# A routing table built with four short VectorE operations per step instead of ScalarE work, and one expert choice that is advanced later

## The chip, the cores and the metric

The kernel runs on one core of a Trainium2 chip. What is measured is device time in microseconds (us), from one launch, on that core; the number compared is the median of three runs. A core has TensorE (PE in the rows below, with PEld for its weight loads), VectorE (DVE), ScalarE (ACT), GpSimd (POOL) and SyncE (SP); each works through its own queue of instructions in order, and they meet at semaphores. SP and POOL issue the DMAs here. Weights and inputs lie in HBM (DRAM), tiles in SBUF, matmul results in PSUM.

## The reference

One decoder layer over 1024 tokens of width 1024. A mixer (gated short convolution, and dilated window attention with 24 heads) is followed by a mixture of 16,384 small experts; the change lies in the second part:

```
def peer_ffn(u, w_query, sub_keys, expert_down, expert_up):
    q = (xf @ w_query).reshape(T, PEER_HEADS, 2, PEER_D_HALF)
    s = jnp.einsum('thcd,hckd->thck', q, sub_keys)
    top_s, top_i = lax.top_k(s, PEER_TOPK)
    cand_s = top_s[:, :, 0, :, None] + top_s[:, :, 1, None, :]
    cand_i = top_i[:, :, 0, :, None] * PEER_N_KEYS + top_i[:, :, 1, None, :]
    best_s, pos = lax.top_k(cand_s, PEER_TOPK)
    idx = jnp.take_along_axis(cand_i, pos, axis=-1)
    gates = jax.nn.softmax(best_s, axis=-1)
    # for each chunk of tokens:
    a = jax.nn.gelu(jnp.einsum('cd,ced->ce', xc, expert_down[ic]), approximate=False)
    return jnp.einsum('ce,ced->cd', gc * a, expert_up[ic])
```

For each token, 8 heads each pick 16 of 16,384 experts. An expert is a row of expert_down (a dot product with the token) and a row of expert_up (added with weight gate times gelu). All of it is float32.

## The kernel before, in words

The 1024 tokens are two halves of 512, and eight tiles of 128. A projection in float32 is three matmuls: each operand is split into a high part (`hi`, rounded by ACT at L165 or L181) and a rest (`lo`, a subtraction on DVE at L167 or L182), and `mm3` (L176 to L178) multiplies hi*hi, hi*lo and lo*hi. So each 512 KB of weights costs one ACT operation and one DVE operation ahead of 24 matmuls of 512 columns.

**The two halves treat the experts differently.** The first half (tiles 0 to 3) gathers rows: `experts()` goes through `STEPS`, (tile, 0) for the down rows and (tile, 1) for the up rows, in the order (0,0), (1,0), (2,0), (0,1), (1,1), (2,1), (3,0), (3,1). A step takes 128 gathers by POOL (L885 or L908), each of one 512 KB block (for 128 tokens, one expert row each) into one of four buffers, and for each gather one DVE operation (L887: dot product; L908's is L910: multiply and add into `acc`). Step (0,1) is different (`summed`): its rows are summed by TensorE (`upacc`, L944) and need no DVE operation per row. In this text this chain is the side chain, and one gather with its DVE operation is a row. The second half (tiles 4 to 7) does not gather: it multiplies by all experts (`dense`). For this it needs a table `g_d` in DRAM that holds, for each token, the gate at each expert that it chose, and zero elsewhere.

**The stages.** Half 0's mixer; half 1's mixer (`mixer(1)`: attention with its projections, the joining of its three groups at L551 to L559, the gates' projections at L611, the merge with `w_attn_out`, `w_conv_out`, `w_out`, then `tail` with the queries); then `dense`: first ten blocks of `hidden` (projection by expert_down and gelu) beside the building of the table; then the main loop of 32 blocks `q`: `weigh(q)` reads the table back as `gg` and multiplies (L1056), and the result is multiplied by the rows of expert_up into PSUM (`held`, `psu`). The last block normalises and writes the output (L1150, L1154, L855). The side chain runs beside all this from half 1's mixer on.

**The choice.** `choose` finds, for one tile of 128 tokens, the experts and gates: 16 columns of scores with MAX, MAX_INDEX and MATCH_REPLACE (L762 to L766), then candidates, ranks and names (L776 to L828), some 174 DVE operations. It is run for eight tiles. `later[1]` to `later[3]` are those of tiles 1 to 3, which the side chain needs before step (t,0). `CHOOSE` = (0, 1, 2, 3) says which of them is advanced where in half 1's mixer: after each head pair of attention group 1 that of tile 1, in group 2 that of tile 2, and in the merge that of tile 3. The columns of a stored tile are read by DMAs that stand in POOL's queue (L839).

**The table.** `build` makes it for one of half 1's tiles, 4 tokens per step, 32 steps per tile, 128 in all. In a step, `oa` (DVE, L1025) marks for 4 tokens which of 128 first keys each choice has; `ob` marks the second key, times the gate; `psg` (TensorE, 4 products) is the table's part for the 4 tokens; ACT copies it into `stg` (L1040, four copies of 128x128), and after 8 steps SP writes 2 MB to `g_d` (four DMAs, L1044). `ob` is made in one of two ways in turn: in even steps ACT takes Abs per token (L1029, four), Relu over all (L1030) and DVE multiplies by the gate (L1031); in odd steps DVE compares (L1033) and ACT multiplies by the gate per token (L1036, four).

**What sets the order.** The program is recorded from generators: the stage's main generator yields amounts of work, and the side chain and the builder are advanced by them (`PACE_B`, `PACE_C`, `PACE_D`, `RATE_G`). A scheduler then orders each engine's instructions from its own estimates, so that the written order is only a tendency. The order that it gives is fixed in the program.

Of the kernel before, what the change touches and what calls it, by code (L numbers as in the profile page):

```python
# [8 lines left out]
F32 = mybir.dt.float32  # L9
# [4 lines left out]
ALU = mybir.AluOpType  # L14
# [28 lines left out]
OBUF = 4  # L43
# [3 lines left out]
CHOOSE = (0, 1, 2, 3)  # L47
# [9 lines left out]
STG = 5  # L57
# [8 lines left out]
def hybrid_layer(ctx, tc, x, xT, pos, rotc, norm_mix, w_proj, w_v, conv_w, w_conv_out, w_attn_out,  # L66
# [805 lines left out]
    def experts():  # L872
        values, turned = {}, {}
        for tt, side_up in STEPS:
# [28 lines left out]
            else:  # L903
                acc = ex.tile([P, D], F32, tag="acc", name="acc")
                SIDE.dma_start(acc, h1_d[r])
                for e in range(P):
                    row = new_row("rowu")
                    G.indirect_dma_start(out=row, out_offset=None, in_=up,  # L908
                                         in_offset=bass.IndirectOffsetOnAxis(ap=idx[:, e:e + 1], axis=0))
                    V.scalar_tensor_tensor(acc, row, a[:, e:e + 1], acc, op0=ALU.mult, op1=ALU.add)  # L910
                    yield 1.0
# [59 lines left out]
    def dense():  # L971
# [28 lines left out]
        def chosen(tt):  # L1000
            if tt == 0:
                yield from later[ORDER[3]]
# [8 lines left out]
        def build(srcs, c0):  # L1011
# [5 lines left out]
                for c in range(c0, c0 + P // TC):  # L1017
                    stg = [den.tile([P, 32, TC], F32, tag="stg", bufs=STG, name="stg") for _ in range(4)]
                    for t4 in range(TC // 4):
# [7 lines left out]
                        if t4 % 2 == 0:  # L1027
                            for t in range(4):
                                S.activation(ob[:, t], iota, AF.Abs, bias=i2[:, t:t + 1], scale=-1.0)  # L1029
                            S.activation(ob, ob, AF.Relu, bias=ones[:, 0:1], scale=-1.0)  # L1030
                            V.tensor_tensor(ob, ob, gv[:, :, None].to_broadcast([P, 4, P]), op=ALU.mult)  # L1031
                        else:
                            V.tensor_tensor(ob, iota[:, None, :].to_broadcast([P, 4, P]),  # L1033
                                            i2[:, :, None].to_broadcast([P, 4, P]), op=ALU.is_equal)
                            for t in range(4):
                                S.mul(ob[:, t], ob[:, t], gv[:, t:t + 1])  # L1036
                        for t in range(4):
                            PE.matmul(ps[:, t], ob[:, t], oa[:, t], start=True, stop=True)  # L1038
                        for w in range(4):
                            S.copy(stg[w][:, :, t4 * 4:t4 * 4 + 4],  # L1040
                                   ps[:, :, 32 * w:32 * w + 32].rearrange("p t i -> p i t"))
                        yield 1.1
                    for w in range(4):
                        nc.sync.dma_start(g_d[c, :, 32 * w:32 * w + 32], stg[w])  # L1044
# [30 lines left out]
        for _ in builder:  # L1075
            yield 0.0
        while "done" not in place:
            next(side)
# [155 lines left out]
```

## Time and profile before

| | |
|---|---|
| median of three runs | 3437.81 us (3435.53 to 3441.62) |
| the profiled execution | 3448.45 us, of which 3446.7 us lie between its first and last instruction |
| PE busy | 3165.5 us (92%) |
| DVE busy | 2669.4 us (77%) |
| ACT busy | 1398.0 us (41%) |
| POOL busy | 1422.7 us (41%) |
| HBM read and written | 885.61 MB and 70.32 MB, 277 GB/s over the span |

Busy shares are means over stages with different limits, so they are read stage by stage: the view of busy time by stretch shows which engine leaves no gap, the view of waits shows who waited for whom there, and the rows of groups give what one instruction of a kind takes. [...]

### The profile page before, as it was taken

Reading aid. Unit: us, or ns where it says so; the run is one execution under the profiler, and the core shown is the slowest. Engines: PE = TensorE matmul, PEld = TensorE weight load, DVE = VectorE, ACT = ScalarE, POOL = GpSimd, SP = SyncE. Lnnn points to the kernel's source line nnn. Section 1 sums busy time; section 2 is a strip of 40 time slices with the busy share of each in tenths; the row PEclk is TensorE's granted clock in tenths of the full one; section 3 lists DMA queues with packets and bytes.
Section 4 is the critical chain, followed back from the end, with each engine's and each line's share of the span. In section 5 each row is a group of like instructions: output and inputs, shape, how many; then the busy total and the mean of one; then the engine's idle time right before and its main releaser. Section 6 shows DMA issues by size and latency. Waiting matters only on the chain.

```text
span 3446.7 us, 45451 instructions
## 1 busy us (share of the span) xinstructions
PE 3165.5 (92%) x15410; PEld 2559.9 (74%) x15410; DVE 2669.4 (77%) x5357; ACT 1398.0 (41%) x2898; POOL 1422.7 (41%) x1101
## 2 busy tenths in 40 slices
PE   7999999999899997979779985699999999999996
PEld 6788788887677875768556764588887878778775
DVE  5333455799999989888987748888887878778887
ACT  3544444543344362333465678332322232222222
POOL 0000000024555455555555334455555656555555
PEclk9999999999999997989889997799999999999998
DMA  4233345778888888999888887999999999999997
GB/s 131 77 118 115 95 136 201 237 251 308 295 297 306 306 304 276 344 321 338 307 295 328 322 316 280 335 341 329 324 347 327 333 330 329 327 322 336 322 318 276
DMA packets 349225, 965.26 MB, mean 280 GB/s; under 512 B 35264, under 2 KB 118720, under 8 KB 346432
## 3 DMA queue, kind: packets, MB, share of 16 engines
q0 software_dynamic: 152064, 551.62, 44.6%
q1 hardware_dynamic: 196928, 410.74, 35.0%
q8 instruction: 121, 1.98, 0.2%
q14 instruction: 112, 0.92, 0.1%
HBM read 885.61 MB, written 70.32 MB: 277 GB/s over the span
## 4 chain that ended last, share of the span: by engine, by line
PE 29%; DMA 16%; issue 14%; DVE 12%; POOL 9%; ACT 2%; SPq 1%; POOLq 0%; DVEq 0%; ACTq 0%
DMA rowu<-in_up,idx 7%; POOL row L885 6%; PE ps L178 5%; PE ps L176 5%; PE ps L177 5%; DMA row<-in_down,idx 4%; DVE row L887 4%; POOL rowu L908 3%; PE held L176 2%; PE held L177 2%; PE held L178 2%; PE psg L1038 2%; DVE lo L167 1%; PE upacc L944 1%; DVE acc L910 1%
## 5 line engine op out<-in xcount | busy, mean ns | idle before, releaser
L885 POOL DMA_INDIRECT row<-in_down,idx x512 | 668.9, 1306 | 670.9 <-DVE a L887 331.2
L908 POOL DMA_INDIRECT rowu<-in_up,idx x384 | 559.1, 1456 | 456.9 <-DVE acc L910 392.8
L165 ACT CAST hi<-raw 128x1024 fp32r<-128x1024 f32 x368 | 387.0, 1052 | 788.3 <-PE ps L177 491.7
L887 DVE CUSTOM_DVE_ANT_0 row<-row,ut 128x1024 f32<-128x1024 f32 x512 | 618.1, 1216 | 94.9 <-DMA row<-in_down,idx 89.3
L167 DVE TENSOR_TENSOR lo<-raw,hi 128x1024 fp32r<-128x1024 f32 x368 | 449.0, 1220 | 259.7 <-ACT hi L165 246.8
L910 DVE SCALAR_TENSOR_TENSOR acc<-rowu,a,acc 128x1024 f32<-128x1024 f32 x384 | 492.4, 1282 | 141.6 <-DMA rowu<-in_up,idx 132.1
L178 PE MATMUL ps<-vhi,lo 128*128 128x512 f32 (+1 forms) x1408 | 531.4, 377 | 29.1 <-DVE lo L167 27.4
L176 PE MATMUL ps<-vhi,hi 128*128 128x512 f32 (+1 forms) x1408 | 527.3, 375 | 5.8 <-ACT ga L989 3.6
L177 PE MATMUL ps<-vlo,hi 128*128 128x512 f32 (+1 forms) x1408 | 526.7, 374 | 0.1
L176 PE MATMUL ps<-uhi,hi 128*128 128x512 f32 x1024 | 407.0, 399 | 7.8 <-ACT hi L165 5.3
L178 PE MATMUL ps<-uhi,lo 128*128 128x512 f32 x1024 | 407.7, 399 | 2.0 <-DVE lo L167 1.9
L177 PE MATMUL ps<-ulo,hi 128*128 128x512 f32 x1024 | 406.7, 397 | 0.5 <-DVE ulo L182 0.5
L178 PEld LDWEIGHTS ps<-vhi,lo 128*128 128x128 f32 x1408 | 267.9, 190 | 84.5 <-DVE lo L167 34.7
L176 PE MATMUL held<-uh,hh 128*128 128x512 f32 x752 | 290.2, 395 | 24.9 <-ACT hh L181 24.9
L176 PEld LDWEIGHTS ps<-vhi,hi 128*128 128x128 f32 x1408 | 268.0, 190 | 54.8 <-ACT ga L989 5.3
L177 PEld LDWEIGHTS ps<-vlo,hi 128*128 128x128 f32 x1408 | 268.1, 190 | 46.7 <-issue 1.2
L177 PE MATMUL held<-ul,hh 128*128 128x512 f32 x752 | 297.1, 395 | 5.3 <-DVE ul L182 5.3
L178 PE MATMUL held<-uh,hl 128*128 128x512 f32 x752 | 294.9, 393 | 0.0
L181 ACT CAST uh<-rawu 128x1024 fp32r<-128x1024 f32 x126 | 131.6, 1049 | 380.6 <-DMA rawu<-in_up_s 310.8
L932 POOL DMA_DIRECT2D acc<-h_d x1 | 0.7, 691 | 619.1 <-DMA h_d<-h 619.1
L176 PEld LDWEIGHTS ps<-uhi,hi 128*128 128x128 f32 x1024 | 193.3, 189 | 54.5 <-ACT hi L165 7.8
L1038 PE MATMUL psg<-oa,ob 128*128 128x128 f32 x1024 | 157.9, 316 | 80.0 <-ACT stg L1040 42.7
(336 smaller groups left out, 5581.2 us busy)
## 6 DMA issues: line engine op xcount, KB each, us to landing
raw<-in_w_proj SPq DMA_DIRECT2D x128, 512.0 KB
raw<-in_down_t SPq DMA_DIRECT2D x128, 512.0 KB
rawu<-in_up_s SPq DMA_DIRECT2D x128, 512.0 KB
g_d<-stg SPq DMA_DIRECT2D x64, 512.0 KB
gg<-g_d SPq DMA_DIRECT2D x32, 1024.0 KB
raw<-in_w_query SPq DMA_DIRECT2D x48, 512.0 KB
raw<-in_w_v SPq DMA_DIRECT2D x24, 512.0 KB
raw<-in_w_out SPq DMA_DIRECT2D x24, 512.0 KB
```

The source lines that it names most:

```text
L165: S.copy(hi, raw)
L167: V.tensor_tensor(lo, raw, hi.bitcast(F32), op=ALU.subtract)
L176: PE.matmul(ps, l[0], r[0], start=first, stop=False)
L177: PE.matmul(ps, l[0], r[1], start=False, stop=False)
L178: PE.matmul(ps, l[1], r[0], start=False, stop=last)
L181: S.copy(hi, src)
L885: G.indirect_dma_start(out=row, out_offset=None, in_=down, in_offset=bass.IndirectOffsetOnAxis(ap=idx[:, e:e + 1], axis=0))
L887: V.tensor_tensor_reduce(out=row, in0=row, in1=ut, scale=1.0, scalar=0.0, op0=ALU.mult, op1=ALU.add, accum_out=a[:, e:e + 1])
L908: G.indirect_dma_start(out=row, out_offset=None, in_=up, in_offset=bass.IndirectOffsetOnAxis(ap=idx[:, e:e + 1], axis=0))
L910: V.scalar_tensor_tensor(acc, row, a[:, e:e + 1], acc, op0=ALU.mult, op1=ALU.add)
L944: m = PE.matmul(part[n][32 * j:32 * j + 32], z[:, j, c0:c0 + 32], rows[j][:, n * TH:n * TH + TH], start=s == 0, stop=s == 31)
L1038: PE.matmul(ps[:, t], ob[:, t], oa[:, t], start=True, stop=True)
```

## The change

`ob` is made by four DVE operations of 128x128, one per token, that compare and multiply by the gate in one go (`tensor_scalar` with the key and the gate as one value per partition each); the ACT operations and the 128x512 DVE operation go. The table's part is copied by two ACT copies of 128x256 instead of four of 128x128, into two buffers per 8 steps instead of four, and written by two DMAs of 1 MB with runs of 8 KB. `OBUF` goes from 4 to 3 and `STG` from 5 to 3 (of double size). In the merge of half 1 tile 3's choice is no longer advanced; the side chain advances it in step (2,1), once every four rows, after the builder has ended.

```
-CHOOSE = (0, 1, 2, 3)
+CHOOSE = (0, 1, 2, 0)
...
                     V.scalar_tensor_tensor(acc, row, a[:, e:e + 1], acc, op0=ALU.mult, op1=ALU.add)
+                    if tt == 2 and e % 4 == 3:
+                        while "built" not in place:
+                            yield 1.0
+                        next(later[3], None)
                     yield 1.0
...
         def chosen(tt):
-            if tt == 0:
-                yield from later[ORDER[3]]
             got = []
...
-                    stg = [den.tile([P, 32, TC], F32, tag="stg", bufs=STG, name="stg") for _ in range(4)]
+                    stg = [den.tile([P, 64, TC], F32, tag="stg", bufs=STG, name="stg") for _ in range(2)]
...
-                        if t4 % 2 == 0:
-                            for t in range(4):
-                                S.activation(ob[:, t], iota, AF.Abs, bias=i2[:, t:t + 1], scale=-1.0)
-                            S.activation(ob, ob, AF.Relu, bias=ones[:, 0:1], scale=-1.0)
-                            V.tensor_tensor(ob, ob, gv[:, :, None].to_broadcast([P, 4, P]), op=ALU.mult)
-                        else:
-                            V.tensor_tensor(ob, iota[:, None, :].to_broadcast([P, 4, P]),
-                                            i2[:, :, None].to_broadcast([P, 4, P]), op=ALU.is_equal)
-                            for t in range(4):
-                                S.mul(ob[:, t], ob[:, t], gv[:, t:t + 1])
+                        for t in range(4):
+                            V.tensor_scalar(ob[:, t], iota, i2[:, t:t + 1], gv[:, t:t + 1], op0=ALU.is_equal, op1=ALU.mult)
...
-                        for w in range(4):
+                        for w in range(2):
                             S.copy(stg[w][:, :, t4 * 4:t4 * 4 + 4],
-                                   ps[:, :, 32 * w:32 * w + 32].rearrange("p t i -> p i t"))
+                                   ps[:, :, 64 * w:64 * w + 64].rearrange("p t i -> p i t"))
...
         for _ in builder:
             yield 0.0
+        place["built"] = True
```

The scheduler gives every engine's order anew. Three places of DVE's order show what moved (L1027 and L1030 are `oa` and `ob` of the changed kernel).

The first place is DVE's order in the building of the table, with few `hidden` projections left. Before:

```order
L167 TENSOR_TENSOR lo<-raw,hi 128x1024
L1025 TENSOR_TENSOR oa<-iota,sT 128x512 x2
L1033 TENSOR_TENSOR ob<-iota,sT 128x512
L1031 TENSOR_TENSOR ob<-ob,sT 128x512
L1025 TENSOR_TENSOR oa<-iota,sT 128x512 x2
L1033 TENSOR_TENSOR ob<-iota,sT 128x512
```

Now, with tile 3's choice or another between:

```order
L1027 TENSOR_TENSOR oa<-iota,sT 128x512
L1030 TENSOR_SCALAR ob<-iota,sT 128x128 x4
L814 TENSOR_TENSOR other<-other,wq 128x256
L765 MAX tv<-sv 128x8
L763 MAX_INDEX ti<-tv,sv 128x8
L811 SCALAR_TENSOR_TENSOR wq<-paf,tif 128x256
L1027 TENSOR_TENSOR oa<-iota,sT 128x512
L1030 TENSOR_SCALAR ob<-iota,sT 128x128 x4
```

A step is one operation of 512 columns and four of 128, where it was two of 512; and operations of a choice stand among the steps up to the end of the building, where before the last choice had ended some 60 steps earlier. Over the whole order, tile 3's choice leaves half 1's attention and gates, and all but 37 of its operations stand ahead of the main loop's first block; of the rows of step (1,1), 41 stand ahead of that block before, and 6 now.

The second place is DVE's order where half 1's attention groups are joined (`n`, `n_t`: the groups' outputs, `pb`: their weights, `e`: of a choice; L887 with one name is the second half of a row's operation). Before:

```order
L887 ISA row,a<-row,ut 128x1024
L887 ISA a 128x1
L557 TENSOR_TENSOR n_t<-n_t,pb 128x512 x2
L182 TENSOR_TENSOR loa<-rawa,hia 128x512
L887 ISA row,a<-row,ut 128x1024
L887 ISA a 128x1
L817 TENSOR_TENSOR e_12320<-e_12320,other 128x256
L887 ISA row,a<-row,ut 128x1024
L887 ISA a 128x1
L559 TENSOR_TENSOR n_7019<-n_7019,n_t 128x512
```

Now:

```order
L167 TENSOR_TENSOR lo<-raw,hi 128x1024
L557 TENSOR_TENSOR n_t<-n_t,pb 128x512 x2
L887 ISA row,a<-row,ut 128x1024
L887 ISA a 128x1
L559 TENSOR_TENSOR n_7019<-n_7019,n_t 128x512
L887 ISA row,a<-row,ut 128x1024
L887 ISA a 128x1
L559 TENSOR_TENSOR n_7019<-n_7019,n_t 128x512
L167 TENSOR_TENSOR lo<-raw,hi 128x1024
```

The joining stood behind the last gate projections, next to `loa` of the merge; now gate projections (L167) still stand among it and behind it.

The third place is the end of DVE's order. Before:

```order
L855 SCALAR_TENSOR_TENSOR h1b_27517<-h1b_27517,sts,nfin 128x512 x2
L204 TENSOR_TENSOR st<-st 128x1
L205 TENSOR_SCALAR st<-st 128x1
L206 TENSOR_TENSOR st<-st 128x1
L855 SCALAR_TENSOR_TENSOR acc<-acc,st,nfin 128x1024
```

Now:

```order
L855 SCALAR_TENSOR_TENSOR h1b_27005<-h1b_27005,sts,nfin 128x512 x2
L910 SCALAR_TENSOR_TENSOR acc<-rowu,a,acc 128x1024 x32
L200 TENSOR_SCALAR st<-st 128x1
L202 RECIPROCAL st<-st 128x1
L203 TENSOR_TENSOR st<-st 128x1
```

Behind the main loop's last output operation stood only the side chain's normalisation; now 32 rows of step (3,1) stand there as well. Counted from the first of the main loop's eight output operations (L855 on `h1b`), 1 row was left before, and 36 are now.

## Rows read from the trace of the kernel before

**Rows 1.** Page, part 4: the chain that ended last, shares by engine.
```profile
PE 29%; DMA 16%; issue 14%; DVE 12%; POOL 9%; ACT 2%; SPq 1%; POOLq 0%; DVEq 0%; ACTq 0%
```

**Rows 2.** Busy time by stretch: us, then PE, PEld, DVE, ACT, POOL, PEclk, DMA, GB/s.
```profile
976.00:1323.00 347.00, 343.55 (x1821) 276.55 (x1820) 329.41 (x912) 169.59 (x303) 176.52 (x146) 1.00 0.89 306
1323.00:1416.00 93.00, 63.77 (x195) 42.46 (x194) 82.81 (x138) 23.71 (x36) 48.81 (x40) 0.72 0.85 293
1686.00:1797.00 111.00, 69.03 (x396) 52.09 (x395) 101.48 (x336) 72.41 (x255) 54.53 (x51) 0.80 0.77 268
1797.00:2018.00 221.00, 211.78 (x1254) 159.93 (x1256) 168.23 (x583) 146.78 (x466) 103.09 (x86) 0.99 0.89 330
2018.00:2198.00 180.00, 100.28 (x610) 81.43 (x602) 121.97 (x158) 124.91 (x474) 84.17 (x67) 0.78 0.82 293
2198.00:3432.00 1234.00, 1198.52 (x5184) 978.15 (x5184) 1014.02 (x1042) 348.94 (x399) 689.06 (x477) 0.99 0.92 328
```

**Rows 3.** Waits, 2018 to 2198 us.
```profile
PE psg L1038 <- ACT stg L1040: 33.9, 14, 6.7
POOL rowu L958 <- PE upacc L944: 22.4, 3, 10.4
```

**Rows 4.** Groups, 1686 to 2198 us: busy us, mean ns | idle before.
```profile
L1040 ACT COPY stg<-psg 128x128 f32<-128x128 f32 x512 | 102.4, 297 | 79.2 <-PE psg L1038 40.3 <-DMA g_d<-stg 18.0 <-remote 13.3
...
L1036 ACT ACTIVATE ob<-ob,sT 128x128 f32<-128x128 f32 x256 | 83.8, 428 | 15.0 <-DVE ob L1033 15.0
L1029 ACT ACTIVATE ob<-iota,sT 128x128 f32<-128x128 f32 x256 | 83.6, 429 | 0.1
```

**Rows 5.** Groups of DVE and ACT, whole run, by shape: busy us, mean ns | idle before.
```profile
L811 DVE SCALAR_TENSOR_TENSOR wq<-paf,tif 128x256 f32<-128x256 f32 x112 | 43.1, 417 | 0.0
...
L798 DVE TENSOR_SCALAR dec<-dec 128x128 f32<-128x128 f32 x8 | 1.8, 220 | 0.1
L257 DVE TENSOR_SCALAR ang<-ang,rc 128x512 f32<-128x512 f32 x2 | 1.0, 486 | 0.0
L259 DVE TENSOR_SCALAR nn<-ang 128x512 f32<-128x512 f32 x2 | 0.8, 422 | 0.0
...
L108 DVE TENSOR_SCALAR band<-diff 128x128 f32<-128x128 f32 x1 | 0.2, 245 | 0.2 <-POOL diff L106 0.2
...
L496 ACT COPY pts<-pt 128x256 f32<-128x256 f32 x32 | 11.4, 375 | 20.5 <-PE pt L490 20.4
```

**Rows 6.** DVE from 2110 us on, in order of time: start us, us.
```profile
2110.19 1.27 DVE L910 SCALAR_TENSOR_TENSOR acc<-rowu,a,acc 128x1024 f32<-128x1024 f32 x1
2111.39 0.68 DVE L1025 TENSOR_TENSOR oa<-iota,sT 128x512 f32<-128x512 f32 x1
2111.99 0.68 DVE L1033 TENSOR_TENSOR ob<-iota,sT 128x512 f32<-128x512 f32 x1
```

**Rows 7.** Waits, 1323 to 1416 us: who waited for whom, us, times, longest.
```profile
ACT ohi L181 <- DVE n L559: 25.2, 4, 13.1
```

**Rows 8.** Groups of DVE, 1323 to 1416 us: busy us, mean ns | idle before.
```profile
L887 DVE CUSTOM_DVE_ANT_0 row<-row,ut 128x1024 f32<-128x1024 f32 x39 | 47.1, 1218 | 4.0 <-DMA row<-in_down,idx 4.0
```

**Rows 9.** POOL in the last 45 us, in order of time.
```profile
3403.63 1.86 POOL L908 DMA_INDIRECT rowu<-in_up,idx  x1 [0.65 <-DVE acc L910]
...
3409.27 0.94 POOL L908 DMA_INDIRECT rowu<-in_up,idx  x1 [0.30 <-issue]
...
3418.85 1.86 POOL L908 DMA_INDIRECT rowu<-in_up,idx  x1 [0.86 <-DVE sts L1154]
...
3427.18 1.68 POOL L908 DMA_INDIRECT rowu<-in_up,idx  x1 [0.30 <-DVE sts L202]
```

**Rows 10.** DVE at the end, in order of time.
```profile
3432.18 1.41 DVE L855 SCALAR_TENSOR_TENSOR h1b<-h1b,sts,nfin 128x512 f32<-128x512 f32 x2
...
3433.71 1.26 DVE L910 SCALAR_TENSOR_TENSOR acc<-rowu,a,acc 128x1024 f32<-128x1024 f32 x1
```

**Rows 11.** Instructions of line 796: durations ns, least, middle and longest.
```profile
L796 DVE TENSOR_SCALAR dec<-paf x8: 209/241/462, 723.6 to 1959.7; 128x128 f32<-128x128 f32 x8
```

More of the change, by code (lines that the diff above doesn't have):

```diff
@@ L42 @@
 SUBS = ((1, 2), (1, 1))
-OBUF = 4
+OBUF = 3
 GATES = 4
@@ L56 @@
 NS = 2
-STG = 5
+STG = 3
 PJ = 3
@@ L1026, in build @@
                                         i1[:, :, None].to_broadcast([P, 4, P]), op=ALU.is_equal)
-                        if t4 % 2 == 0:
-                            for t in range(4):
-                                S.activation(ob[:, t], iota, AF.Abs, bias=i2[:, t:t + 1], scale=-1.0)
-                            S.activation(ob, ob, AF.Relu, bias=ones[:, 0:1], scale=-1.0)
-                            V.tensor_tensor(ob, ob, gv[:, :, None].to_broadcast([P, 4, P]), op=ALU.mult)
-                        else:
-                            V.tensor_tensor(ob, iota[:, None, :].to_broadcast([P, 4, P]),
-                                            i2[:, :, None].to_broadcast([P, 4, P]), op=ALU.is_equal)
-                            for t in range(4):
-                                S.mul(ob[:, t], ob[:, t], gv[:, t:t + 1])
+                        for t in range(4):
+                            V.tensor_scalar(ob[:, t], iota, i2[:, t:t + 1], gv[:, t:t + 1], op0=ALU.is_equal, op1=ALU.mult)
                         for t in range(4):
                             PE.matmul(ps[:, t], ob[:, t], oa[:, t], start=True, stop=True)
-                        for w in range(4):
+                        for w in range(2):
                             S.copy(stg[w][:, :, t4 * 4:t4 * 4 + 4],
-                                   ps[:, :, 32 * w:32 * w + 32].rearrange("p t i -> p i t"))
+                                   ps[:, :, 64 * w:64 * w + 64].rearrange("p t i -> p i t"))
                         yield 1.1
-                    for w in range(4):
-                        nc.sync.dma_start(g_d[c, :, 32 * w:32 * w + 32], stg[w])
+                    for w in range(2):
+                        nc.sync.dma_start(g_d[c, :, 64 * w:64 * w + 64], stg[w])
         def weigh(q):
```

## The prediction

> **What bounds the kernel now.** I read the chain of waits first, then busy time by stretch, then the waits inside the stretches that the change touches. The chain [rows 1] has no single owner: PE 29%, DMA 16%, issue 14%, DVE 12%, POOL 9%. So the end is set by two things that finish together, the matmuls of the main path and the side chain of rows (one gather by POOL and one DVE operation each). That must be kept in mind: to make the main path shorter alone is worth nothing if the side chain does not follow.
>
> The stretches [rows 2] have different limits. From 976 to 1323 us (attention and gates of half 1) PE is busy 343.6 and DVE 329.4 of 347: both are full. From 1323 to 1416 (joining of the groups, start of the merge) PE is busy only 63.8 of 93 at a clock of 0.72, and DVE 82.8 of 93. From 1686 to 1797 (the building begins) DVE is full with 101.5 of 111. From 1797 to 2018 PE is (211.8 of 221). From 2018 to 2198 neither is: PE 100 of 180, DVE 122, ACT 125. There PE's products wait 33.9 us for ACT's copies `stg` [rows 3]: the remainder of the table is made at ACT's pace. From 2198 to 3432 PE is full, 1198.5 of 1234.
>
> **Part 1: ACT is relieved.** Per pair of steps ACT loses four L1029 (429 ns), four L1036 (428) and one Relu, and the 512 copies of 297 ns become 256 of 128x256, for which the nearest row says 375 [rows 4, 5]. The copies fall from 102 to about 96 us, the rest (83.6 + 83.8 and the Relus) goes. ACT is then no limit in this stage. What is late next is DVE.
>
> **Part 2: DVE gets more work per step.** The removed operation is 128x512: 0.68 us long, and the next one starts 0.60 later [rows 6], so 128 x 0.60 = 77 us go. The four new ones are 128x128 with two values per partition. The same operation without them is 0.220 to 0.245 long, thus about 0.14 apart; one such value adds 486 - 422 = 64 ns [rows 5]. Whether the second costs another 64 the trace does not show: 0.20 (one counts) to 0.27 (both), and 0.14 if they are hidden. I take 0.235, between the two nearest: 512 x 0.235 = 120 us, +43 over the stage (+26 to +61; -5 at 0.14).
>
> [...]
>
> **Part 3: tile 3's choice.** All groups between L762 and L828 come to 423 us for eight choices, the largest of them being L811 [rows 5]: 53 per tile, and with starts 0.06 to 0.08 nearer than the durations over some 174 operations about 42 us of DVE. They leave the stretch 976 to 1416. In DVE's order, row operations of the side chain fill their place in the attention, and the joining moves up among the gate projections: in the part that answers to 1323 to 1416 about 19 of 39 rows are gone, 19 x 1.22 = 23 us [rows 8], and about as much of the joining stands ahead of it. There ACT waited 25.2 us for `n` of DVE [rows 7], so DVE decided. DVE's work there thus falls from 83 to some 40 us, and PE needs some 45 (195 matmuls at the main loop's 1198.5 / 5184 = 0.23 us [rows 2]); I take 58 for 93, since DMA waits of 10 or more remain: **-35**. Bounds: -15 if rows come late there, -48 if all but PE's 45 is hidden.
>
> The choice now lies in the building stage: 137 of its 174 operations, 33 us. In exchange 35 of 41 rows of step (1,1) leave that stage, 35 x 1.20 = 42 us [rows 6]. For the stage: -77 + 120 + 33 - 42 = +34 us of DVE. By the places in DVE's order this falls unevenly:
> - 1686 to 1797: about +18. DVE is full, so it counts, less the few us in which it waited: **+14** (+8 to +25).
> - 1797 to 2018: about +29, to 197 of 221. PE stays the limit, with six more steps to do than before: **+4** (-10 to +15).
> - 2018 to 2198: about -13, to 109. ACT's pace is gone, so DVE's 109 at 93% full is 117, and 14 are left of the 20 us in which all wait for the last table part to go to DRAM and come back: 131 for 180, **-49** (-35 to -60).
>
> Three waits are moved or changed. The columns of tile 3 are loaded by DMAs in POOL's queue, which now stand among the gathers of step (0,1); a load waits until DVE is done with an earlier column, and behind it wait gathers, and behind these TensorE's `upacc`. POOL waited 22.4 us for `upacc` here [rows 3], which covers it; without that cover up to that much is lost. The new wait for "built" costs nothing, as step (2,1) is reached only in the main loop. The two-buffer copies still wait at each chunk's start for the chunk before; ACT waited 18.0 us for that in all [rows 4], and is now idle enough.
>
> The 37 operations left over stand in the main loop's first blocks, about 9 us where DVE is nearly full: **+8** (+3 to +12).
>
> **Part 4: the rows that left come back at the end.** In the main loop the order locks rows to blocks, some 25 to 37 per two blocks before and now, so a lag at its start is a lag at its end. At its first output operation 1 row is left before and 36 now. What one row takes with little beside it is read at the end: twelve gathers from 3403.63 to 3427.18 are 23.55 / 12 = 1.96 us apart, the last four distances 2.08 [rows 9]. Lower bound: a gather of 0.94 and 0.30 to the next [rows 9], 1.24; DVE needs 1.20. At the very end gathers took 1.68 to 1.86 beside DVE's rows, so I take 1.96. Then 36 x 1.96 = 71 us, plus 11 from the last row to the end, against 3446.7 - 3432.2 = 14.5 before [rows 10]: **+67** (+41 to +72). PE is idle meanwhile.
>
> **Sum.** -35 + 14 + 4 - 49 + 8 + 67 = **+9 us**. Against the profiled execution's 3448.5 this is 3457; it lies 10.6 above the median of the runs, so in their terms 3437.8 + 9 = **3447**. It is a small difference between a gain of about 85 in two places and losses of about 93, and the sign is not safe.
>
> **The rivals.**
> 1. The gain wins. The new operations are 0.20 apart (stretches +8, -8, -55) and rows at the end, with no weights loading beside them, come every 1.5 us: 54 + 11 - 14.5 = 50. Sum: -35 + 8 - 8 - 55 + 5 + 50 = -35, 3403. For it: POOL's short gathers of 0.94. Against it: the gathers of 1.68 to 1.86 at the very end, when PE was done.
> 2. DVE becomes the limit of the whole building stage, because its operations and POOL's gathers hold each other up. L796, an operation of the new kind, took 209 to 462 ns [rows 11]. If each of step (0,1)'s 128 gathers delays DVE by 462 - 209 = 0.25 us, 32 us of DVE are added, and no gain is left in 1797 to 2198 but some 20: 3447 + 30 = 3477. At 0.07 us per gather it already adds 9 us, as much as the whole forecast. [...]
> 3. The choice's departure gives nothing, because PE is full up to 1323 anyway and the joining's chain of DMA, ACT and PE keeps its 93 us: 3447 + 30 = 3477. Against it speaks the 25.2 us wait for DVE.
>
> That the choice does not reach the up stage is no rival but seen in the order: nearly all of it stands in the building stage.
>
> **How the numbers follow.** Forecast (the sum within about 20 us) 0.42, rival 1 0.27, rival 2 0.19, rival 3 0.12. 0.2%, some 7 us, is about what a measurement of this kernel can tell from no change. Of the forecast's 0.42 I give 0.06 to faster by more than that, 0.19 to the same, 0.17 to slower. So faster 0.33, same 0.19, slower 0.48. The predicted time is 3447. Cases of both signs are likely; the forecast's own range is 3430 to 3466. The range for 8 in 10 takes in most of the rivals: 3405 to 3478.
>
> **What would show it.** In the profile after: (a) L1029, L1030 and L1036 on ACT are gone and `stg` copies are about 375 ns; (b) the four-operation line on DVE has a spacing of 0.20 to 0.27; (c) the stretch in which the groups are joined is about 35 us shorter, and PE's clock dip there smaller; (d) the main loop's first L1056 starts some 60 us earlier than 2198; (e) after the last `h1b` operation 32 L910 follow at about 2 us, with PE at zero. The prediction is wrong if the main loop itself changes length (1234 us), if the rows at the end are much nearer than 1.96 us, or if the stage from the first `oa` to the first L1056 is not 25 to 40 us shorter.

## The result, and the profile after

The changed kernel takes 3465.59 us (median of five runs, 3455.15 to 3468.14), the kernel before 3437.81 (five runs). The ratio is 1.0065 (95% interval 1.0047 to 1.0082): slower by 0.65%. The forecast was 3447 with 3405 to 3478. The changed kernel's profiled execution took 3457.54 us (span 3455.8), 9.1 more than that of the kernel before; the sum on record said +9. But the medians lie 27.8 us apart: the changed kernel's profiled execution is the second shortest of its five runs, and that of the kernel before lay 10.6 above its median. So the sum fits this one pair of executions, and is 19 us short of the medians.

How much single executions differ can be read from later traces. Four of the kernels below (without the last 36 rows, with seven and with six row buffers, with fewer weight buffers) give DVE the same operations in the same order as the changed kernel up to the main loop (but for at most the last 26 of some 4600). Its main loop started at 2130.1 us, theirs at 2139.8, 2149.3, 2151.0 and 2149.7. A start of the main loop in one trace is thus known to some 20 us, and the changed kernel's own trace is the earliest of the five.

The page's part 4, the chain that ended last by engine (compare [rows 1]):

```profile
DMA 10%; issue 9%; POOL 8%; DVE 2%; POOLq 0%; ACT 0%; DVEq 0%
```

PE, which had 29%, does not stand in it. But these shares add up to 29% of the span only: here the chain can be followed back to 2485 us, before the change to 606. Over the same stretch at the end, from 3000 us on, it looks like this before and after (by line; the view breaks off its lines):

```profile
by line: DMA rowu<-in_up,idx 34.6%; issue 33.8%; POOL rowu L908 11.4%; POOL row L885 10.3%; DVE acc L910 4.3%; DMA row<-in_down,idx 1.8%; DVE row L887 0.8%; DVE h1b L1150 0.7%; DVE hl L182 0.5%; DVE ul L182 0.5%; DVE rest L1146 0.2%; POOLq
by line: DMA rowu<-in_up,idx 34.0%; issue 31.8%; POOL row L885 14.5%; POOL rowu L908 10.4%; DVE acc L910 4.5%; DMA row<-in_down,idx 1.9%; DVE lo L167 0.5%; DVE h1b L1145 0.3%; DVE ul L182 0.3%; DVE h1b L855 0.2%; POOLq L885 0.1%; DVE rest L
```

Both are POOL's gathers, the way of a row to its buffer and DVE's row operations; PE has nothing in either. So in the last 450 us the side chain already set the end before the change; the prediction's two things that finish together were read from [rows 1], a mean over most of the span, which does not show this. From 2500 to 3000 us PE still had 25% of the chain before, and has none now.

Busy time by stretch, cut at the same instructions as [rows 2] (columns as there; the last two stretches are the main loop up to just before the first `h1b` operation, and what comes behind the last `h1b` operation):

```profile
976.00:1339.00 363.00, 352.42 (x1863) 279.29 (x1862) 326.77 (x731) 154.19 (x300) 199.08 (x155) 1.00 0.90 311
1339.00:1393.00 54.00, 43.94 (x171) 33.60 (x171) 43.59 (x68) 19.99 (x30) 27.19 (x22) 0.94 0.95 351
1665.00:1788.00 123.00, 91.01 (x448) 69.11 (x447) 122.69 (x436) 32.01 (x84) 58.22 (x53) 0.71 0.77 272
1788.00:2008.00 220.00, 217.44 (x1268) 161.26 (x1268) 198.00 (x799) 77.47 (x169) 98.47 (x93) 1.00 0.91 343
2008.00:2130.00 122.00, 82.94 (x542) 59.95 (x540) 110.31 (x407) 40.41 (x110) 34.05 (x36) 0.89 0.72 268
2130.00:3371.00 1241.00, 1201.04 (x5184) 977.52 (x5184) 1024.05 (x1080) 347.63 (x399) 710.06 (x475) 0.99 0.92 325
3384.00:3443.00 59.00, 0.00 (x0) 0.00 (x0) 39.04 (x32) 0.00 (x0) 39.66 (x30) 0.50 0.82 280
```

The stretch behind the last gate projection took 54 us for 93, the last part of the building 122 for 180, and the main loop started at 2130 instead of 2198. PE's last product ends at 3358.5 us, 97 us before the end; before the change it was 27 us (3419.6).

The building's groups (1665 to 2130 us, against [rows 4]):

```profile
L1030 DVE TENSOR_SCALAR ob<-iota,sT 128x128 f32<-128x128 f32 x512 | 144.4, 345 | 1.2 <-ACT sT L1018 1.1
...
L1034 ACT COPY stg<-psg 128x256 f32<-128x256 f32 x256 | 83.5, 376 | 181.5 <-PE psg L1032 168.1 <-issue 10.5 <-DMA g_d<-stg 2.6
```

A `stg` copy takes 376 ns, as the row of L496 in [rows 5] had said (375). ACT now waits 168 us for the products (40 before, [rows 4]). One step in DVE's timeline:

```profile
2062.33 0.66 DVE L1027 TENSOR_TENSOR oa<-iota,sT 128x512 f32<-128x512 f32 x1
2062.92 1.10 DVE L1030 TENSOR_SCALAR ob<-iota,sT 128x128 f32<-128x128 f32 x4
2063.95 0.67 DVE L1027 TENSOR_TENSOR oa<-iota,sT 128x512 f32<-128x512 f32 x1
```

Four new operations take 2063.95 - 2062.92 = 1.03 us, thus 0.257 each; the forecast had 0.235, with 0.20 to 0.27 as bounds.

The waits of 2008 to 2130 us (against [rows 3]):

```profile
POOL out L856 <- DVE cand L782: 35.0, 1, 35.0
POOL rowu L962 <- PE upacc L948: 21.5, 4, 10.8
...
PE psg L1032 <- ACT stg L1034: 2.3, 4, 0.7
```

PE's wait for ACT's copies has gone from 33.9 to 2.3 us (that of its weight loads from 38.1 to 13.3), POOL's wait for `upacc` has stayed. New is the first line. L856 is the output DMA of step (0,1), in POOL's queue ahead of the gathers of step (1,1), and it waits for the normalisation of that step (L200 to L855). Before, the normalisation took 6.5 us of DVE's timeline (2074.0 to 2080.5) and POOL waited 7.8. Now it takes 27.5 (2075.2 to 2102.7), because each of its six small operations stands behind steps of the table and operations of the choice.

The end, in POOL's timeline (against [rows 9]):

```profile
3378.40 0.94 POOL L908 DMA_INDIRECT rowu<-in_up,idx  x1 [1.50 <-DVE sts L205]
...
3440.19 0.94 POOL L908 DMA_INDIRECT rowu<-in_up,idx  x1 [1.03 <-DVE acc L910]
3442.49 0.57 POOL L918 DMA_DIRECT2D nfin<-in_final_norm  x1 [1.36 <-DVE acc L910]
```

Between the first and the last of these 31 gathers lie 30 distances: 61.79 / 30 = 2.06 us a row, with PE idle. The way of one row there: until it has landed 4.9 to 7.6 us (middle 5.6), then DVE's operation of 1.28. From the gather's start to the end of that operation, when its buffer is free, it is 7.2 on the mean, and with four buffers 4 x 2.06 = 8.2 to the start of the next gather into it.

### The profile page after: what moved, and what is told of

Read it like the earlier page. It is cut to its first block, busy times and chain, and to the rows that moved or that the text cites. A ratio compares the mean times of both kernels' runs of the same rounds, so it can differ in the third digit from the quotient of the medians.

```text
span 3455.8 us, 44940 instructions
## 1 busy us (share of the span) xinstructions
PE 3168.6 (92%) x15410; PEld 2549.9 (74%) x15410; DVE 2721.8 (79%) x5741; ACT 1180.9 (34%) x2051; POOL 1441.4 (42%) x1101
## 5 line engine op out<-in xcount | busy, mean ns | idle before, releaser
L885 POOL DMA_INDIRECT row<-in_down,idx x512 | 675.9, 1320 | 657.8 <-DVE a L887 352.7
L908 POOL DMA_INDIRECT rowu<-in_up,idx x384 | 576.1, 1500 | 430.4 <-DVE acc L910 335.7
L887 DVE CUSTOM_DVE_ANT_0 row<-row,ut 128x1024 f32<-128x1024 f32 x512 | 618.1, 1217 | 126.3 <-DMA row<-in_down,idx 121.9
L167 DVE TENSOR_TENSOR lo<-raw,hi 128x1024 fp32r<-128x1024 f32 x368 | 448.6, 1219 | 244.7 <-ACT hi L165 231.4
L178 PE MATMUL ps<-uhi,lo 128*128 128x512 f32 x1024 | 408.3, 399 | 10.6 <-DVE lo L167 10.4
L178 PEld LDWEIGHTS ps<-uhi,lo 128*128 128x128 f32 x1024 | 193.7, 189 | 59.4 <-DVE lo L167 17.9
```

The costliest lines, as they stand in the source:

```text
L167: V.tensor_tensor(lo, raw, hi.bitcast(F32), op=ALU.subtract)
L178: PE.matmul(ps, l[1], r[0], start=False, stop=last)
L885: G.indirect_dma_start(out=row, out_offset=None, in_=down, in_offset=bass.IndirectOffsetOnAxis(ap=idx[:, e:e + 1], axis=0))
L887: V.tensor_tensor_reduce(out=row, in0=row, in1=ut, scale=1.0, scalar=0.0, op0=ALU.mult, op1=ALU.add, accum_out=a[:, e:e + 1])
L908: G.indirect_dma_start(out=row, out_offset=None, in_=up, in_offset=bass.IndirectOffsetOnAxis(ap=idx[:, e:e + 1], axis=0))
```

## The experiments

Each ratio is to the kernel before on the same chip. The kernel before itself took 3438 to 3458 us there (medians of 3438.8, 3450.5, 3452.9 and 3458.0), so ratios are compared and not times. Times from traces are those of one profiled execution, and starts of the main loop carry the 20 us named above.

**The table part alone** (builder_only). `CHOOSE` and `chosen` as before, no advance in step (2,1):

```
-CHOOSE = (0, 1, 2, 0)
+CHOOSE = (0, 1, 2, 3)
```

> Only the table part of the change: four DVE operations per step for ob, two copies, 8 KB runs; tile 3's choice stays in half 1's merge as before. Theory L (locked rows: each microsecond that the main path gains before its main loop is a microsecond of rows that comes back behind it): the joining of the groups keeps its 93 us, the last part of the building is 45 to 60 us shorter, and about 32 rows stand behind the first h1b operation, 2.06 us each, so 66 + 11 - 14.5 = +62; sum about +5 to +17 against the kernel before, 3443 to 3455. Theory S (one stall: in the changed kernel the normalisation that ends step (0,1), L200 to L855, took 27 us of DVE's queue where it was 6.5 us, because DVE had become the limit of the building, and POOL's queue stood behind it for 35.0 us at L856): the stall is here too, 20 us or more from L200 to L855 of that step, since it comes from the table part; the time is then near the changed kernel's, 3450 to 3465. If the stall comes from tile 3's choice among the steps, it is under 10 us here and the time is 3425 to 3440.

Measured: 3460.42 us, 1.0053 (1.0027 to 1.0078). The stall is here too: 19.6 us from L200 to the end of L855, and POOL waits 21.4 at L856 (theory S had said 20 or more). The main loop starts at 2144.9, 53 of the 68 us earlier, and 32 rows stand behind the first `h1b` operation. The table part by itself brings most of the main path's gain, and nearly all of the loss.

**The choice alone** (choice_only). The kernel before with `CHOOSE` = (0, 1, 2, 0) and the advance in step (2,1).

> Only the choice of tile 3 is moved; the table is made as before, by ACT and DVE. Theory L: the joining is some 25 us shorter (measured in the changed kernel: 23 by its end), ACT still limits the building, the main loop starts 10 to 25 us earlier, and 8 rows stand behind the first h1b operation: 8 x 2.06 + 11 - 14.5 = +13; sum 0 to -10 against the kernel before, 3428 to 3438. Theory S: DVE has free time in the building (before it waited for ACT and PE), so the normalisation that ends step (0,1) takes under 12 us; the time is at most that of the kernel before, 3415 to 3438. Rival (the choice among the steps makes the stall): over 20 us from L200 to L855, and 3445 or more.

Measured: 3440.53 us, 1.0018 (0.9996 to 1.0039), the same as before, where both theories had it somewhat faster. The normalisation takes 8.4 us, so the choice among the steps makes no stall by itself. The main loop starts at 2179.3, 18.5 earlier, which is no more than two executions of one order can differ; 8 rows stand behind the first `h1b` operation.

**A way round the stall** (acc_own). A sum buffer of its own for step (0,1), its output in SP's queue:

```
-                acc = ex.tile([P, D], F32, tag="acc", name="acc")
+                acc = m8.tile([P, 2, D], F32, tag="big", name="acc0")[:, 0]
                 yield from summed(*turned[tt], acc, r)
...
-            finish(acc, r, st, nfin, SIDE)
+            finish(acc, r, st, nfin, nc.sync if tt == SUMMED else SIDE)
```

> The changed kernel, with a sum buffer of its own for step (0,1) (from the pool of the large tiles) and its output DMA in SP's queue: rows of step (1,1) need not wait for the normalisation that ends step (0,1), which is left where it is. Theory S: POOL's 35.0 us wait at L856 goes, 23 rows stand behind the first h1b operation where 36 were, and the time falls by some 13 x 2.06 = 27 us against the changed kernel (3457 in its profiled execution, 3466 median): 3430 to 3442. Theory L: the stall is only one form of the time that is missing, DVE has no room for rows before the building ends, so what is saved at the stall is lost in the main loop: within 8 us of the changed kernel, 3452 to 3470.

Measured: 3465.18 us, 1.0068 (1.0047 to 1.0088): nothing gained. The wait at L856 is gone and 23 rows instead of 36 stand behind the first `h1b` operation, but the main loop starts at 2160.1, 30 us later than in the changed kernel's trace and 9 later than the latest of the five with its order. DVE's timeline shows what took the place:

```profile
2120.52 1.28 DVE L910 SCALAR_TENSOR_TENSOR acc<-rowu,a,acc 128x1024 f32<-128x1024 f32 x1
2122.49 0.67 DVE L1027 TENSOR_TENSOR oa<-iota,sT 128x512 f32<-128x512 f32 x1
2123.08 1.11 DVE L1030 TENSOR_SCALAR ob<-iota,sT 128x128 f32<-128x128 f32 x4
2124.11 0.68 DVE L1027 TENSOR_TENSOR oa<-iota,sT 128x512 f32<-128x512 f32 x1
2124.71 1.11 DVE L1030 TENSOR_SCALAR ob<-iota,sT 128x128 f32<-128x128 f32 x4
2125.74 0.68 DVE L1027 TENSOR_TENSOR oa<-iota,sT 128x512 f32<-128x512 f32 x1
2126.34 1.11 DVE L1030 TENSOR_SCALAR ob<-iota,sT 128x128 f32<-128x128 f32 x4
2127.36 1.28 DVE L910 SCALAR_TENSOR_TENSOR acc<-rowu,a,acc 128x1024 f32<-128x1024 f32 x1
```

One row for every three steps, and each pushes the steps back. The stall was real, but taking it away gained nothing. That the time given to the rows there is taken from the main path fits the timeline; the next run shows it more clearly.

**More rows beside the building** (acc_own_spread), on top of this: `RATE_G` 0.8 for 1.3, `PACE_C` 1.2 for 1.75.

> As acc_own, and the building is spread over more of the blocks beside it (RATE_G 0.8 for 1.3) with more rows drawn beside them (PACE_C 1.2 for 1.75). In the order 5 rows stand behind the first h1b operation. Theory S: the main path keeps most of its gain of 62 us (main loop's first block at 2130 to 2150 us) and the tail is 5 x 2.06 + 11 = 21 us where it was about 82: 3395 to 3420. Theory L: rows that stand earlier lengthen the building by about 2 us each, so the main loop begins at 2175 to 2200 and the time is 3430 to 3450.

Measured: 3479.56 us, 1.0112 (1.0069 to 1.0155), slower than every forecast. 5 rows stand behind the first `h1b` operation, but the main loop starts at 2220.1, 69 to 90 us later than in the five executions with the changed kernel's order: what 31 rows saved behind it was lost ahead of it, and more. The slower pace of the building has a part in this that was not separated.

**Half of the steps back to ACT** (half_act). In odd steps `ob` as in the odd steps of the kernel before:

```
+                        if t4 % 2 == 0:
                             for t in range(4):
                                 V.tensor_scalar(ob[:, t], iota, ...)
+                        else:
+                            V.tensor_tensor(ob, iota..., i2..., op=ALU.is_equal)
+                            for t in range(4):
+                                S.mul(ob[:, t], ob[:, t], gv[:, t:t + 1])
```

> The changed kernel, but in every second step ob is made as in the odd steps of the kernel before: one DVE comparison of 128x512 (0.60 us of DVE's queue) and four multiplications by ACT, where the four new operations take 4 x 0.2575 = 1.03. DVE has 64 x 0.43 = 27 us less to do in the building, ACT some 64 x 4 x 0.33 = 84 us more, of the 190 us that it has idle there. Theory D (since the change, DVE is the limit of the building's two ends: main path, choice and rows share it, so that a row put there delays the main path as much as it saves later, as acc_own showed): the building is 15 to 27 us shorter, no fewer rows are done in it, and the time falls by 15 to 35 against the changed kernel (3466 median): 3430 to 3450. Theory L (locked rows: what the main path gains comes back as rows at the end): within 8 us of the changed kernel, 3457 to 3473. Rival: ACT is the limit again, 3465 to 3490.

Measured: 3470.81 us, 1.0062 (1.0041 to 1.0084), the same as the changed kernel. Theory D falls: with 27 us less on DVE the main loop starts at 2154.4, later than in each of the five executions with the changed kernel's order (2130.1 to 2151.0), if by as little as 3 us. PE waits for ACT again (waits, 2015 to 2160 us):

```profile
PEld psg L1038 <- ACT ob L1036: 13.9, 12, 1.9
PE psg L1038 <- ACT ob L1036: 10.7, 10, 1.8
```

The two overlap, since the weight loads run beside the products (from 2019 to 2154 us PE is busy 86.2 us and PEld 67.9, together more than the 135). In the whole building PE waits 25.1 us for ACT's `ob` here and 11.8 for DVE's, where it waited 33.5 for DVE's in the changed kernel. So relief for DVE is paid with a wait for ACT; that this wait alone cancels it was not tested. Five more rows also stand ahead of the main loop here (497 gathers left for 502).

**The copies without the new operations** (copies_only). The changed kernel with `ob` as before.

> The changed kernel with ob made as in the kernel before (ACT and DVE in turn); the two copies, the 8 KB runs and the moved choice stay. Against choice_only (3441 median) it tells the two copies apart, against the changed kernel the new operations of DVE. Theory D: DVE has 43 us less than in the changed kernel, ACT is the limit of the end of the building again, but with a copy's time of 0.75 per step where it was 1.19: 3420 to 3440, and 5 rows or so behind the first h1b operation. Rival (the copies are not what held ACT): within 5 us of choice_only, 3436 to 3446. Theory L has nothing else to say here than for choice_only, 3430 to 3441.

Measured: 3463.31 us, 1.0043 (1.0026 to 1.0059), no faster than the choice alone. The main loop starts at 2196.3, as before the change (2197.8), 45 to 66 us later than in the five executions with the changed kernel's order. The two copies and the 8 KB runs bring nothing measurable; the earlier main loop comes with the new operations of DVE, in which ACT has no part (and with fewer rows ahead of it: 470 gathers are left here, 502 in the changed kernel).

**What the rows at the end cost.** The last 36 rows of step (3,1) left out:

```
-                for e in range(P):
+                for e in range(P - 36 if tt == 3 else P):
                     row = new_row("rowu")
```

> The changed kernel without the last 36 rows of step (3,1): these 36 of 128 experts of tile 3 are left out of its sum. It prices the tail by itself. My prediction's part 4 says 36 x 2.06 us = 74 of the changed kernel's 3457 (profiled execution) are these rows: 3384 to 3396, with the last output DMA as the end. If the tail hides something else of 20 us or more (PE's last products, the normalisation, the output DMAs), 3405 or more.

Measured: 3406.84 us in its one run, above the expected 3384 to 3396. But the kernel before took 3450.54 there: the ratio is 0.9873, against 1.0065 for the changed kernel, which makes some 66 us for the tail, inside the 61 to 74 that were expected. By the times alone it is 51, and counted from the start of the main loop in both traces 60 (3455.8 - 2130.1 against 3405.1 - 2139.8). With one run it stays between these.

**Six row buffers.** From the main loop on; room from the split weights:

```
-UPS = 7
+UPS = 5
...
         bld.close()
+        more = ctx.enter_context(tc.tile_pool(name="more", bufs=2))
+        spare.extend([more] * 2)
```

> The changed kernel with six row buffers where it had four, from the main loop on; the room is taken from the split weights (5 buffers where there were 7). It asks what sets a row's price. If it is the way of a row through its buffer (gather, 5.4 to 7.5 us until the row has landed, 1.28 for DVE; over four buffers that is the 2.06 measured at the end), six buffers give about 1.5 to 1.6 at the end, in the order 20 rows stand behind the first h1b operation, and the tail falls from 82 to some 43 us: 3415 to 3430 if the main loop keeps its 1241 us. If the main loop has no room for more rows (DMA at 325 GB/s, DVE and PE full), it grows by what the tail loses: 3450 to 3470. If five weight buffers are too few, the main loop grows by more: 3470 to 3500.

Measured: 3398.3 us, 0.9848 (0.9814 to 0.9881): 1.5% faster than the kernel before, and faster than every case of the expectation, which had not let the main loop get shorter (from its first L1050 to the first `h1b` operation it took 1207.3 us for 1242.5). The page's part 4 by engine:

```profile
PE 38%; DVE 3%; issue 3%; DMA 2%; POOL 1%; ACT 0%; another core or an unknown queue 0%; POOLq 0%; DVEq 0%; ACTq 0%; SPq 0%
```

PE is back in the chain: from 3000 us on it has 85% of it, where it had none.

**The weight buffers alone** (u5: `UPS` = 5, four row buffers) part the two edits:

> The changed kernel with five buffers of split weights where it had seven, and four row buffers as before. It parts the two edits of the kernel with six row buffers. In the order 20 rows stand behind the first h1b operation, as there. Theory R: the row buffers did it; with four, rows at the end stay 2.06 us apart and DVE still waits some 250 us or more for rows: ratio to the kernel before 0.998 to 1.010. Rival (the later weights did it, by leaving DMA and DVE to the rows): 0.985 to 0.992.

Measured: 3472.85 us, 1.0063 (1.0037 to 1.0090), the same as the changed kernel. The two kernels are alike in the building (main loop from 2149.7 and from 2151.0) and in the rows behind the first `h1b` operation (20 and 20). Their main loops, from the first L1050 to the first `h1b` operation, are 1264.6 and 1207.3 us long. With four row buffers, busy time of the main loop and DVE's group of rows in it:

```profile
2150.00:3414.00 1264.00, 1211.53 (x5184) 985.69 (x5184) 1049.10 (x1095) 350.84 (x400) 708.79 (x492) 0.98 0.92 327
```
```profile
L910 DVE SCALAR_TENSOR_TENSOR acc<-rowu,a,acc 128x1024 f32<-128x1024 f32 x357 | 458.1, 1283 | 133.4 <-DMA rowu<-in_up,idx 121.7 <-DMA acc<-h_d 6.5 <-DVE lo L167 0.6
```

With six:

```profile
2151.00:3358.00 1207.00, 1193.31 (x5184) 975.04 (x5184) 1048.79 (x1087) 349.53 (x400) 706.77 (x494) 0.99 0.95 342
```
```profile
L910 DVE SCALAR_TENSOR_TENSOR acc<-rowu,a,acc 128x1024 f32<-128x1024 f32 x361 | 463.6, 1284 | 21.2 <-DMA rowu<-in_up,idx 15.4 <-DVE acc L910 0.4
```

The same matmuls, nearly the same number of POOL's operations (492 and 494) and the same DVE busy time. What is missing is DVE's wait for rows that had not landed, 121.7 against 15.4 us (and 45.0 against 11.4 at L887, in 2150 to 3380): DVE works in order, and behind its wait stand the operations that feed PE. PE's waits for DVE's half of the split weights in the two main loops, with four row buffers and with six:

```profile
PE held L177 <- DVE ul L182: 38.3, 18, 5.5
PE held L177 <- DVE ul L182: 5.6, 8, 2.1
```

Not all of DVE's time is won: with six it waits 66.8 us for ACT's `hi` at L167 (7.7 with four), and ACT in turn for PE. The DMAs move 342 GB/s instead of 327.

**Six in the kernel before, seven in the changed one, six with the table part alone:**

> The kernel before with the same six row buffers and five buffers of split weights from the main loop on. Theory R (four row buffers set the pace of the rows in the main loop, and DVE, which works in order, stands still for rows that have not landed: 227 us in the kernel before, 276 in the changed one, 98 in the changed one with six): DVE's waits for rows fall under 120 us here too and the main loop gets 20 to 30 us shorter, but the building still goes at ACT's pace, so that the changed kernel with six buffers (ratio 0.985) stays ahead by 25 to 60 us: ratio 0.990 to 1.000. Rival (the change to the table and the choice is worth nothing with room for rows either): ratio 0.980 to 0.988.

> The changed kernel with seven row buffers and four buffers of split weights (six and five: ratio 0.985). Theory R: in the order 8 rows stand behind the first h1b operation where 20 did; 12 fewer at some 1.5 us are 18 us less at the end: ratio 0.978 to 0.982. Rival: four buffers hold two pairs of weights at a time, PE waits for ACT's and DVE's split at each block: 0.985 or more. Price of a row at the very end by the way through the buffers: 8.2 / 7 = 1.2, by the DMAs (512 KB at 345 to 360 GB/s) 1.5: I expect 1.5, no nearer than with six.

> Only the table part of the change (the choice of tile 3 stays in the merge), with six row buffers and five of split weights in the main loop. It parts what the two halves of the change are worth once rows have room: without either the ratio is 0.994, with both 0.985. Theory R: the choice's departure makes the joining some 25 us shorter, and costs 8 to 15 us in the building and the first blocks, so it is worth 10 to 17 us: ratio 0.988 to 0.991 here. If the choice is worth nothing in the end (its operations are only moved to where DVE is as scarce): 0.983 to 0.987. If nearly all of the gain is the choice's: 0.992 or more.

| | median, us | ratio (95% interval) |
|---|---|---|
| before, six row buffers | 3428.78 | 0.9936 (0.9915 to 0.9957) |
| table part alone, six | 3400.07 | 0.9834 (0.9805 to 0.9863) |
| changed, six | 3398.3 | 0.9848 (0.9814 to 0.9881) |
| changed, seven | 3391.19 | 0.9831 (0.9793 to 0.9870) |

Six buffers alone give the kernel before 0.6%, as theory R expected. With them the table part is worth a further 1.0% (0.9936 to 0.9834). The choice's departure shows no gain with six row buffers, and none with four (builder_only against the changed kernel); the intervals leave room for 10 to 15 us either way. With six, the joining ends 21 us earlier, and the building gives that back: the main loop starts at 2148.7 without the move and at 2151.0 with it. So the expectation of 0.988 to 0.991 was wrong. The seventh buffer cannot be told from the sixth, and its ratio lies just above the expected 0.978 to 0.982; DVE's waits for `rowu` are 17.8 us in the whole run with six and 0.7 with seven, so little was left to gain there.

## Why the prediction was right, and where it was off

**Point by point.** (a) Right: ACT's operations gone, copies 376 ns. (b) 0.257, in the bounds, near the upper one: 512 x 0.022 = 11 us more DVE than taken. (c) The stretch is 39 us shorter (forecast 35), with 20 rows in it for 39 ([rows 8]) and a granted TensorE clock (PEclk, a share of full speed) of 0.94 for 0.72. But it no longer holds the joining: all operations of L557 and L559 now stand ahead of it, among the gate projections (the last one at 1317.9 us), and with them went ACT's wait for `n`. The attention got 16 longer for it. PE has 9 us more to do there (1863 matmuls for 1821 [rows 2], 12 of them the `pb` products of the joining), and its idle time grew from 3.4 to 10.6, because it waits for `lo`, a wait that did not exist there before:

```profile
PE ps L178 <- DVE lo L167: 8.1, 10, 2.0
```

DVE does the joining and 154 rows there, where it did 139 rows, and it waits 34.8 us for rows that had not landed (6.7 before). Net -23 where -35 was forecast. The step that failed in part 3 is the one that took the gain of the shorter stretch without asking what the joining costs where it went. (d) The first L1050 stands at 2130.1, 68 us earlier (forecast 60): 1686 to 1797 became 12 longer (+14), 1797 to 2018 is unchanged (+4), the rest 58 shorter (-49). (e) Right: 36 rows behind the first `h1b` operation, 2.06 us apart for 1.96. From that operation to the end it took 83.1 us for 14.5, +69 for +67. The main loop up to it is 8 us longer, the forecast's +8.

**How much of the fit is luck.** The terms measured -23, +12, -1, -58, +8 and +69, with +2 between the stretches: +9. The joining was 12 us worse than forecast and the end of the building 9 better, so the two largest errors nearly cancel. The prediction's own last sign fired: from the first `oa` to the first L1050 the stage is 46 us shorter (452.7 for 498.9), outside the 25 to 40. And the pair of traces flatters the sum, since the changed kernel's main loop starts up to 21 us later in the other executions with its order; the medians say +28 and the ratio +22. So the mechanism of the prediction held (main path earlier, rows left over behind it at about 2 us each), the range held, and the match to the microsecond is chance.

**The rivals.** Rival 1 (rows every 1.5 us) did not happen: 2.06. With six buffers the last nine gathers of the changed kernel start 12.62 / 8 = 1.58 apart, so with four neither POOL nor DVE had been the limit there, and the short gathers spoke for what was possible, not for what would be. Rival 2: L1030 took 327, 336 and 553 ns (least, middle, longest) with a mean of 345. 40 of its 512 operations took 404 ns or more, the others at most 375; beside 39 of the 40 a gather of POOL was under way when they began, and they ended 43 to 58 ns behind its end. So holds of DVE by gathers are there but rare, 39 in 512; of the eight operations of [rows 11] three took 401 to 462 ns beside such a gather. The 9 ns between middle and mean are all that this could have cost the new operations, 512 x 9 ns = 5 us. Rival 3 was wrong for the stretch of the joining and right in the end: the choice's departure brought no gain that could be measured.

**The size of the new operation.** A `TENSOR_SCALAR` of 128 columns took 220 ns without values per partition (L798, [rows 5]) and 336 with two (L1030). 336 - 220 = 116 is nearly twice the 64 ns that one such value was seen to add [rows 5]; against the single L108, which like the new operation does two things to each element, it is 336 - 245 = 91. In both readings the second value is not free.

**What the prediction read right but not deeply enough** is part 4. It said that the order ties rows to blocks and that a lag at the start of the main loop is a lag at its end. The runs give the price, and show what changes it. From the first L1050 to the last gather, divided by the gathers in between:

| kernel | row buffers | first L1050 (before: L1056), us | gathers left | last gather, us | us per gather |
|---|---|---|---|---|---|
| before | 4 | 2197.8 | 468 | 3427.2 | 2.63 |
| changed | 4 | 2130.1 | 502 | 3440.2 | 2.61 |
| table part alone | 4 | 2144.9 | 497 | 3439.3 | 2.60 |
| choice alone | 4 | 2179.3 | 475 | 3414.6 | 2.60 |
| acc_own | 4 | 2160.1 | 491 | 3447.7 | 2.62 |
| acc_own_spread | 4 | 2220.1 | 471 | 3465.2 | 2.64 |
| half_act | 4 | 2154.4 | 497 | 3453.4 | 2.61 |
| copies_only | 4 | 2196.3 | 470 | 3440.3 | 2.65 |
| u5 | 4 | 2149.7 | 502 | 3449.1 | 2.59 |
| before | 6 | 2185.5 | 503 | 3408.0 | 2.43 |
| changed | 6 | 2151.0 | 503 | 3384.5 | 2.45 |
| table part alone | 6 | 2148.7 | 503 | 3373.7 | 2.44 |
| changed | 7 | 2149.3 | 501 | 3369.5 | 2.44 |

With four buffers the rest of the program up to the last gather is the number of gathers left times 2.6 us (2.59 to 2.65), whatever was done ahead of it. The 2.6 is a mean over the main loop, some 2.65 in the changed kernel, and the rows behind it at 2.06. The change started the main loop 67.7 us earlier and left 34 more gathers: 34 x 2.61 = 89, less 67.7 and 8 for the slightly lower price, is +13 at the last gather; behind it 19.5 us followed before and 15.6 now, which makes the +9. This is the account of the pair of traces and no second proof. Read the other way round: before the change the building took these 34 rows along in 67.7 us, 2.0 us each, and now they cost 2.6. It also fits that rows drawn forward did not help: put into the full building a row costs the main path about as much (acc_own_spread: 31 gathers fewer, 69 to 90 us later, 2.2 to 2.9 each).

What is not settled is which of PE (1193 of 1207 us busy with six) and the DMAs (0.95 busy at 342 GB/s) is the limit with six and seven buffers. The best kernels of these are 1.7% faster than the kernel before, and cannot be told from each other: the table part with six row buffers, and the whole change with seven.

## What to carry to other kernels

Where two chains end together and one engine serves both in order, count what the other chain still has to do at the point where the first one gains, and multiply by its own price per item; if that is more than the gain, look for what sets the price (here the number of buffers in a ring) before the work is made shorter. An edit that only moved work of a full engine to another place where it is full was worth nothing here, however much shorter one stretch became. A stall that stands out in the waits is not yet the cause: taken away, it gained nothing here. Shares of the chain that ended last are compared over the same stretch, and starts in single traces with what two executions of one order differ by.

## What the runs showed of the hardware

- A `tensor_scalar` of 128x128 float32 on DVE takes 336 ns with two values per partition and 220 (one operation) to 245 (two) with none: 91 to 116 ns for the two. Four in a row start 0.257 us apart.
- Gathers of 512 KB through four buffers came every 2.06 us with PE idle, at 280 GB/s, and the last nine through six buffers every 1.58. Beside the full main loop 2.6 fell to 2.44 us, and the DMAs moved 342 GB/s where it was 327: with four, the number under way had held them back.
- Room for two more gathers changed an engine that had nothing to do with them: in the main loop DVE's waits for rows fell by 140 us (121.7 and 45.0 to 15.4 and 11.4), PE's waits for DVE's `ul` by 33 (38.3 to 5.6), and the loop's length by 57.
- Executions with the same order on DVE reached the main loop up to 21 us apart (2130.1 to 2151.0), 1% of the way.
